# Routing with its maxima in the PSUM, high parts of the first experts beside it, two low parts moved, and filler products on TensorE

## The chip, the core and the metric

One program runs on one core of a Trainium2 chip: TensorE (PE, with its weight loads PEld), VectorE (DVE), ScalarE (ACT), GpSimd (POOL) and the queues that issue DMAs (SP's above all; ACT and POOL issue some). The metric is the time of one execution in microseconds (us); lower is better. Several executions are timed, and one more is recorded by the profiler.

## What is computed

One decoder layer: a mixer (sparse attention beside a gated linear recurrence) for 512 prompt tokens and 8 sample tokens, and behind it a mixture of 16 gated MLPs. Only the second half matters here. Cut to it:

```
h  = rms_norm(x, g_pre_ffn) * (1 + sc_f) + sh_f
pg = softmax(h @ w_rg + b_rg)                 # 4 groups of 4 experts
g_star, pg_top = argmax(pg), max(pg)
le_g = (h @ w_re + b_re) of the group g_star  # 4 logits
top_v, top_i = top_k(le_g, 2)
w_top = softmax(top_v) * pg_top               # weights of the two experts
y  = sum over the two experts e: ((silu(h @ w_gate[e]) * (h @ w_up[e])) * w) @ w_down[e]
x  = x + gt_f * rms_norm(y, g_post_ffn)
```

A token has 1024 features, an expert 256 hidden ones, so an expert's weights are 3 MB in fp32.

## The kernel before

The mixer's end runs in five token tiles of 128 (the last holds the 8 samples). `after(t, ...)` does the residual, the norm and the router's logits of tile t. Tile 3 is the last. Its final two DVE instructions are line 1376, which writes the 20 logits of each token into `LG`, and line 1377, which makes the tile's normalised rows `mg` (128x1024) for the copy `H2` in HBM, from which the experts gather.

**Routing** stands between this and the experts and runs on small tiles of 128 partitions (token in tile) by 5 tiles by a few values. `first_max` (lines 1468 to 1472) finds the first maximum in each set of four: the maximum, a comparison with it, a product with falling numbers `r4v`, its maximum, a comparison again. It is called twice (best, then second best). Line 1481 takes the best out before the second call. `OH` and `C` are the chosen experts as ones and zeros; 20 small products on TensorE with the triangle `tri` and the ones `onb` (line 1490) make every token's rank in its expert; ten products (line 1548, 16 rows) and one (line 1554) turn these into the list `gi` of rows for each expert, which GpSimd's indirect DMA (line 1615) uses to gather up to 96 rows of `H2` into a tile `XG`. The same ten products with 48 rows follow for the tokens' weights `wt`. ACT blanks the `XG` tiles (line 1575) before they are gathered into, and makes two exponentials (1480, 1498). `who` tells which expert comes at which place; SP reads it and then issues loads for experts from the fourth on.

**Experts.** TensorE multiplies fp32 as three products of a high and a low part (hi*hi, hi*lo, lo*hi). So each loaded weight tile of 128x1024 (a part: four of gate and up, two of down, numbered 6w to 6w+5 for expert w) is cut by `split`: ACT copies it to the high part (line 112), DVE or POOL subtracts that to get the low part (line 113). `split_upto(n)` cuts parts up to n. The first SOON = 4 are cut beside the routing, with their low parts on POOL; parts 4 to 7 just before the first expert, with DVE. `entry()` transposes a gathered tile on TensorE (line 1628) and splits it into `xh`, `xl`; `gate_up` is 24 products of 512 columns into one PSUM bank (line 1640); `gated`, `turned`, `down` follow.

The routing and the expert phase run in an order written by hand (`tc.manual_schedule`; for the experts the string ORD_M, where S cuts a part, G is `gate_up`, A `gated`, E `entry`, T `turned`, F `down` and the scatter, B a bit of bookkeeping, K a gather). Each engine works through its own queue in that order. Weight loads go to 28 slots; a load is issued as soon as a slot is free.

Of the kernel before, what the change touches and what calls it, by code (L numbers as in the profile page):

```python
# [39 lines left out]
HI = 12  # L40
POOLK = (2, 4, 6)
PRE = 2
SOON = 4
ONDVE = (0, 3)
CUT = (2, 4, 6)
BOOK = 0
# [18 lines left out]
def body(tc, I, O):  # L65
# [22 lines left out]
    def ps_mm():  # L88
        return bank("mm", 2, 512)
# [18 lines left out]
    def v2(t):  # L108
        return t.rearrange("p (h n) -> p h n", h=2)

    def split(src, hi, lo, eng=None):
        act.activation(hi, src, AF.Copy)  # L112
        (eng or dve).tensor_tensor(lo, src, hi.bitcast(F32), op=ALU.subtract)  # L113
# [1238 lines left out]
    def after(t, n, A, B, C, cw):  # L1352
        fast = dve if t == 3 else pool
        m = x1[t]
        xr = aft.tile([128, D], F32, name="xr", bufs=2)[:n]
        sp.dma_start(xr, I["xp"][t] if t < 4 else I["xs"])
        mg, tg = (aft.tile([128, D], F32, name=nm, bufs=2)[:n] for nm in ("mg", "tg"))
        ss = aft.tile([128, 4], F32, name="ssa", bufs=2)[:n]
        A = A()
        for hf in range(2):  # L1360
            c = slice(512 * hf, 512 * hf + 512)
            act.activation(tg[:, c], m[:, c], AF.Square, accum_out=ss[:, hf:hf + 1])
            (dve if t == 3 and hf else pool).tensor_tensor(mg[:, c], m[:, c], A[:, hf], op=ALU.mult)
        dve.tensor_scalar(ss[:, 0:1], ss[:, 0:1], 1.0 / D, EPS, op0=ALU.mult, op1=ALU.add)
        act.activation(ss[:, 1:2], ss[:, 1:2], AF.Sqrt, scale=1.0 / D, bias=ss[:, 0:1])
        dve.reciprocal(ss[:, 1:2], ss[:, 1:2])
        for hf in range(2):
            c = slice(512 * hf, 512 * hf + 512)
            dve.scalar_tensor_tensor(m[:, c], mg[:, c], ss[:, 1:2], xr[:, c], op0=ALU.mult, op1=ALU.add)
        sp.dma_start(X1[t, 0:n], m)  # L1370
        yield
        pool.tensor_tensor(v2(tg), v2(m), B(), op=ALU.mult)
        mixed[t] = act.activation(mg, m, AF.Square, accum_out=ss[:, 2:3])
        lg_ = router(tg if t == 4 else m, n, wrt if t == 4 else wrb)
        r = rstd(ss[:, 2:3])
        dve.scalar_tensor_tensor(LG[0:n, t], lg_, r, cw, op0=ALU.mult, op1=ALU.add)
        dve.scalar_tensor_tensor(v2(mg), v2(tg), r, C(), op0=ALU.mult, op1=ALU.add)
        sp.dma_start(H2[128 * t:128 * t + n], mg)

    def all_after():  # L1380
# [37 lines left out]
    def split_upto(n, lo_on=lambda c: pool if c in LOP else dve):  # L1418
        while st.cutup < n:
            i = st.cutup  # L1420
            assert i < HI or (i - HI) in used or st.over, "overwritten too early"
            load_upto(i + 1)
            at[i] = left.pop(0)
            parts[i] = high[i % HI], ring[at[i]](F32R)
            s_, raw = raws.pop(i)
            split(raw, *parts[i], lo_on(i % 6))
            left.append(s_)
            st.cutup += 1

    def source(w):  # L1430
        if w >= EARLY:
# [3 lines left out]
    tc.keep_in_program_order(act.preload_act_table_set("exp_and_others"))  # L1435
    with tc.issue_after(mixed[3].ins):
        split_upto(SOON, lambda c: pool)
    s_af.close()
    s_nsa.close()
    s_w = stage()  # L1440
# [8 lines left out]
    def small(name, *shape, dt=F32):  # L1449
        return rt.tile([128, 5, *shape], dt, name=name)  # L1450
# [2 lines left out]
        return x.unsqueeze(2).to_broadcast([128, 5, 4])  # L1453

    eg, sg_, e2 = small("eg", 4), small("sg_"), small("e2", 4)
    sets = [rt.tile([128, 25, 4], F32, name=f"sets{q}") for q in range(3)]
    mxs = [rt.tile([128, 25], F32, name=f"mxs{q}") for q in range(3)]
    C = small("C", 4, 4, dt=BF)

    def b25(x):  # L1460
# [5 lines left out]
    def first_max(x, m, oh):  # L1466

        dve.tensor_reduce(m, x, axis=AX.X, op=ALU.max)
        dve.tensor_tensor(oh, x, b25(m), op=ALU.is_equal)
        dve.tensor_tensor(oh, oh, r4v, op=ALU.mult)  # L1470
        dve.tensor_reduce(mxs[2], oh, axis=AX.X, op=ALU.max)
        dve.tensor_tensor(oh, r4, b25(mxs[2]), op=ALU.is_equal)

    lg25 = LG.rearrange("p t (g e) -> p (t g) e", e=4)
    route = tc.manual_schedule(engines={dve.engine, act.engine})
    route.__enter__()
    first_max(lg25, mxs[0], sets[0])
    mxg = mxs[0].rearrange("p (t g) -> p t g", t=5)
# [9 lines left out]
    for t in range(6):  # L1488
        for q in range(min(t, 4) + 1 if t < 5 else 5):
            pe.matmul(pr[:, 16 * t:16 * t + 16], tri if q == t else onb, C[:, q].rearrange("p g e -> p (g e)"),  # L1490
                      start=(q == 0), stop=(q == t or q == 4))
    pr = pr[:, 0:96].rearrange("p (t e) -> p t e", t=6)
    OHE = OH.rearrange("p q t g e -> p q t (g e)")
    dve.tensor_tensor(mxs[1], mxs[1], mxs[0], op=ALU.subtract)
    dve.tensor_tensor(e2, mxs[1].rearrange("p (t g) -> p t g", t=5)[:, :, 1:5], ohg, op=ALU.mult)
# [90 lines left out]
    pw = ps_t()  # L1586
    pe.matmul(pw[0:1, 0:16], kpos[0:16, 98:99], place[0:16, 0], start=True, stop=True)
    dve.tensor_copy(who, pw[0:1, 0:16])
    for q in range(2, NXG):
        blank(q)  # L1590
    weights()
# [132 lines left out]
    def fetch_upto(n):  # L1724
        while st.fetch < min(n, len(units)):
            c = units[st.fetch][1]
            fetch(gi[:, c:c + 1])
# [13 lines left out]
    with tc.manual_schedule(engines=MANUAL and {getattr(nc, e).engine for e in MANUAL}):  # L1741
        with tc.issue_after(routed[0].ins), tc.issue_after(routed[1].ins):
            fetch_upto(NXG)
            split_upto(6 + PRE)
        x, old, k = entry(), [], dict.fromkeys("GAEFTK", 0)
        fetch_upto(NXG + 1)
        for o in ORD_M:
            u = k[o] if o in k else 0
# [233 lines left out]
```

## Time and profile before

| | us |
|---|---|
| median of 3 runs (lowest to highest) | 790.48 (789.93 to 792.44) |
| the profiled execution's own time | 791.27 |
| its span, first to last instruction | 789.6 |
| busy in the span: PE, DVE, ACT, POOL | 651.7, 464.0, 374.1, 183.3 |

The profiled execution is 0.79 us above the median. Times in the rows below are from the span's start. TensorE's granted clock has two levels here, 1.0 (2.4 GHz) and 0.5 (1.2 GHz).

### The profile page before, as it was taken

The page shows a single profiled execution, that of the slowest core. Times are in us where ns is not written, and L with a number is a line of the kernel's source. Part 1 is how long each engine was busy: PE and PEld are TensorE (multiplying, and loading weights), DVE is VectorE, ACT ScalarE, POOL GpSimd, SP SyncE. Part 2 cuts the span into 40 slices and gives each one's busy share as a digit, 9 for nine tenths or more (in the row PEclk, how much of TensorE's full clock was granted, in tenths as well). Part 3 has the DMA queues.
Part 4 walks back from the last instruction along what each step waited for, and adds up shares of the span by engine and source line. Part 5 has one row for each costly group of instructions (what it writes and reads, how often), then busy time and mean ns, then how long its engine had stood idle before and what let it go on. Part 6 is the DMA issues. An engine that isn't in the chain of part 4 may idle for free. (4 is left out here: it accounts for less than half of the span.)

```text
span 789.6 us, 13169 instructions
## 1 busy us (share of the span) xinstructions
PE 651.7 (83%) x4495; PEld 490.3 (62%) x4495; DVE 464.0 (59%) x1140; ACT 374.1 (47%) x759; POOL 183.3 (23%) x208
## 2 busy tenths in 40 slices
PE   3885988998999999897999739995288899999930
PEld 1663866687878788885676426564255577666620
DVE  4523613345867765577643544356865976888806
ACT  4212512334455547623444234445445766888723
POOL 1000310002130131425432112435301223222114
PEclk9898999999999999999999958997588999999975
DMA  8876798866454632106221485338698889998515
GB/s 302 262 256 218 258 315 295 316 197 205 141 175 130 182 118 73 56 4 262 94 81 55 102 303 177 112 123 319 212 358 295 263 222 287 359 333 296 148 29 213
DMA packets 74604, 160.81 MB, mean 204 GB/s; under 512 B 11346, under 2 KB 39538, under 8 KB 74146
## 3 DMA queue, kind: packets, MB, share of 16 engines
q1 hardware_dynamic: 59844, 125.98, 46.6%
q10 hardware_dynamic: 10654, 25.39, 9.9%
q0 software_dynamic: 4032, 8.53, 5.1%
q8 instruction: 37, 0.61, 0.3%
q14 instruction: 37, 0.30, 0.1%
HBM read 145.29 MB, written 24.28 MB: 215 GB/s over the span
## 5 line engine op out<-in xcount | busy, mean ns | idle before, releaser
L563 PE MATMUL pp<-hhi,wh 128*128 128x260 f32 x256 | 75.6, 295 | 0.3 <-ACT kvt L441 0.3
L563 PE MATMUL pp<-hlo,wh 128*128 128x260 f32 x256 | 74.4, 291 | 0.0
L563 PE MATMUL pp<-hhi,wl 128*128 128x260 f32 x256 | 74.2, 290 | 0.0
L1669 POOL DMA_INDIRECT Y<-ot,gi x17 | 24.4, 1438 | 130.1 <-ACT ot L1668 123.0
L563 PEld LDWEIGHTS pp<-hhi,wh 128*128 128x128 f32 x256 | 49.4, 193 | 2.7 <-issue 2.0
L563 PEld LDWEIGHTS pp<-hhi,wl 128*128 128x128 f32 x256 | 49.3, 193 | 2.4 <-issue 2.3
L563 PEld LDWEIGHTS pp<-hlo,wh 128*128 128x128 f32 x256 | 49.4, 193 | 1.4 <-issue 1.2
L655 ACT ACTIVATE jn<-P,M 128x128 bf16<-128x128 f32 (+3 forms) x64 | 35.9, 560 | 27.3 <-DVE M L653 21.8
L113 DVE TENSOR_TENSOR wl<-wr,wh 128x1024 fp32r<-128x1024 f32 x9 | 11.2, 1250 | 39.8 <-ACT wh L112 39.8
L1058 ACT ACTIVATE PT<-mm 128x256 f32<-128x256 f32 x80 | 23.9, 388 | 19.8 <-PE mm L1054 19.7
L1640 PE MATMUL pf<-ewi,xh 128*96 128x512 f32 x72 | 30.2, 419 | 2.0 <-ACT xh L112 2.0
L653 DVE CUSTOM_DVE_ANT_0 P<-mm,tb 128x128 f32<-128x128 f32 (+3 forms) x64 | 29.0, 483 | 4.0 <-PE mm L646 3.9
L397 PE MATMUL mm<-hhi,wh 128*128 128x260 f32 x144 | 29.9, 288 | 1.3 <-ACT wh L112 1.3
L1640 PE MATMUL pf<-ewi,xl 128*96 128x512 f32 x72 | 29.5, 409 | 1.2 <-DVE xl L113 1.2
L112 ACT ACTIVATE wh<-wr 128x1024 fp32r<-128x1024 f32 x9 | 9.5, 1057 | 43.3 <-DMA wr<-in_wi 25.9
L397 PE MATMUL mm<-hlo,wh 128*128 128x260 f32 x144 | 30.0, 285 | 0.0
L397 PE MATMUL mm<-hhi,wl 128*128 128x260 f32 x144 | 29.7, 287 | 0.0
L646 PE MATMUL mm<-ka,qs 128*128 128x512 f32 (+2 forms) x112 | 27.6, 354 | 0.1
L1054 PE MATMUL mm<-qs,ka 128*128 128x512 f32 x80 | 26.6, 405 | 0.0
L1667 ACT ACTIVATE ot<-mm 96x512 f32<-96x512 f32 x17 | 10.1, 594 | 33.3 <-PE mm L1664 33.3
L397 PEld LDWEIGHTS mm<-hhi,wh 128*128 128x128 f32 x144 | 22.2, 188 | 5.0 <-issue 3.4
L299 PEld LDWEIGHTS po<-cg,w1c 128*128 128x128 f32 x160 | 21.5, 214 | 5.7 <-issue 3.3
(651 smaller groups left out, 1885.1 us busy)
## 6 DMA issues: line engine op xcount, KB each, us to landing
ewr<-in_ew SPq DMA_DIRECT2D x37, 512.0 KB
wa<-in_wa SPq DMA_DIRECT2D x16, 1024.0 KB
wr<-in_wi ACTq DMA_DIRECT2D x25, 512.0 KB
ewt<-in_ew SPq DMA_DIRECT2D x24, 512.0 KB
cg<-in_cc SPq DMA_DIRECT2D x64, 128.0 KB
ewh<-in_ew SPq DMA_DIRECT2D x16, 512.0 KB
x<-in_ew SPq DMA_DIRECT2D x15, 512.0 KB
mh<-in_wa SPq DMA_DIRECT2D x13, 512.0 KB
```

Of the source, the lines that this page charges most:

```text
L113: (eng or dve).tensor_tensor(lo, src, hi.bitcast(F32), op=ALU.subtract)
L299: pe.matmul(p[:, 128 * k:128 * k + 128], w1c[:, k, s, :], cg[:, :, k, s, :], start=(s == 0), stop=(s == 7))
L397: pe.matmul(p[:, hf, 0:260], a[:, k, :], b[:, k, hf * 260:hf * 260 + 260], start=(k == 0 and j == 0), stop=(k == KT - 1 and j == 2))
L563: pe.matmul(p[:, 0:260], a[:, k, :], b[:, k, c], start=(k == 0 and j == 0), stop=(k == KT - 1 and j == 2))
L646: pe.matmul(o, QS[g][:, h % 4, qc], KA[g][:, j, a:b], start=(j == 0), stop=(j == 1))
L653: dve.tensor_tensor_reduce(out=p, in0=sb[:, br], in1=tb0[:, 384 - 128 * i:512].rearrange("p (k n) -> p k n", n=128), scale=SL[h], scalar=1 ...
L655: act.activation(jn[:, 0:128 * (i + 1)], p.rearrange("p k n -> p (k n)"), AF.Exp, scale=-1.0, bias=M[:, 0, i, br, h:h + 1], accum_out=M[:, ...
L1054: pe.matmul(S[:, br], KS[g][:, q, br, j], QS[g][:, :, qc], start=False, stop=(q == 1))
L1058: act.activation(PT[:, :, h], S4[:, :, h], AF.Exp, scale=-SL[4 * g + h])
L1640: pe.matmul(pg, a[:, k, :], b[:, wk_], start=(k == 0 and j == 0), stop=(k == 7 and j == 2))
L1667: act.activation(o3[:, 0], pd[:, 0], AF.Copy)
L1669: pool.indirect_dma_start(out=Y, out_offset=bass.IndirectOffsetOnAxis(ap=gix, axis=0), in_=ot, in_offset=None, bounds_check=T - 1, oob_is_ ...
```

## The change

```diff
-SOON = 4
+SOON = 2
+SOONH = 6
+WARM = (5, 7, 3)
 ...
# after(t, ...)
+        if t == 3:
+            gcp = ps_mm()
+            act.activation(gcp, GC, AF.Copy)
 ...
-        dve.scalar_tensor_tensor(v2(mg), v2(tg), r, C(), op0=ALU.mult, op1=ALU.add)
+        dve.scalar_tensor_tensor(v2(mg), v2(tg), r, gcp if t == 3 else C(), op0=ALU.mult, op1=ALU.add)
 ...
# split_upto(n, lo_on)
+            high_part(i)
             s_, raw = raws.pop(i)
-            split(raw, *parts[i], lo_on(i % 6))
+            lo_on(i % 6).tensor_tensor(parts[i][1], raw, parts[i][0].bitcast(F32), op=ALU.subtract)
 ...
+    made = set()
+
+    def high_part(i):
+        if i not in made:
+            made.add(i)
+            load_upto(i + 1)
+            act.activation(high[i % HI], raws[i][1], AF.Copy)
 ...
         split_upto(SOON, lambda c: pool)
+        for i in range(SOON, SOONH):
+            high_part(i)
 ...
+    tabs = ps_f()
-    mxs = [rt.tile([128, 25], F32, name=f"mxs{q}") for q in range(3)]
+    mxs = [tabs[:, 0:25], rt.tile([128, 25], F32, name="mxs1"), tabs[:, 25:50]]
+    r4p = tabs[:, 128:228].rearrange("p (g e) -> p g e", e=4)
 ...
# first_max(x, m, oh)
-        dve.tensor_tensor(oh, oh, r4v, op=ALU.mult)
+        dve.tensor_tensor(oh, oh, r4p, op=ALU.mult)
 ...
+    junk = ps_mm().rearrange("p a b -> p (a b)")
+    def kept_up(n):
+        for _ in range(n):
+            pe.matmul(junk[:, 0:512], onb, tri.unsqueeze(1).to_broadcast([128, 4, 128]), start=True, stop=True)
+    act.activation(r4p, r4v, AF.Copy)
-    route = tc.manual_schedule(engines={dve.engine, act.engine})
+    route = tc.manual_schedule(engines={dve.engine, act.engine, pe.engine})
 ...
+    kept_up(WARM[0])        # behind the 20 rank products
 ...
+    kept_up(WARM[1])        # behind the product for `who`
 ...
             fetch_upto(NXG)
+            split_upto(SOON + 1)
+            x, old, k = entry(), [], dict.fromkeys("GAEFTK", 0)
+            kept_up(WARM[2])
             split_upto(6 + PRE)
-        x, old, k = entry(), [], dict.fromkeys("GAEFTK", 0)
```

In words: the two maxima that `first_max` writes and the numbers `r4v` that it reads lie in one PSUM bank, and for tile 3 ACT copies the table `GC` into the PSUM, from where line 1377 reads it. POOL makes two low parts beside the routing, not four; DVE makes the other two later. ACT makes six high parts beside the routing, not four. TensorE gets 5, 7 and 3 products of 512 columns whose result nobody reads. The first `entry()` comes ahead of the cutting of parts 3 to 7. How the engines' orders change shows at three places.

DVE in the routing, from line 1377 on (`tab` is the table `GC` in the SBUF, `mm` and `pf` are PSUM banks, `sets` and `mxs` SBUF tiles, `kon` and `r4v` constants in the SBUF). Before:

```order
L1377 SCALAR_TENSOR_TENSOR mg<-tg,ssa,tab_5472 128x1024
L1468 TENSOR_REDUCE mxs_6122<-LG 128x25
L1469 TENSOR_TENSOR sets_6119<-LG,mxs_6122 128x100
L1470 TENSOR_TENSOR sets_6119<-sets_6119,r4v 128x100
L1471 TENSOR_REDUCE mxs_6124<-sets_6119 128x25
L1472 TENSOR_TENSOR sets_6119<-kon,mxs_6124 128x100
L1479 TENSOR_TENSOR eg<-LG,mxs_6122 128x20
L1481 SCALAR_TENSOR_TENSOR sets_6120<-sets_6119,LG 128x100
```

The same place of the change:

```order
L1382 SCALAR_TENSOR_TENSOR mg<-tg,ssa,mm 128x1024
L1487 TENSOR_REDUCE pf<-LG 128x25
L1488 TENSOR_TENSOR sets_6120<-LG,pf 128x100
L1489 TENSOR_TENSOR sets_6120<-sets_6120,pf 128x100
L1490 TENSOR_REDUCE pf<-sets_6120 128x25
L1491 TENSOR_TENSOR sets_6120<-kon,pf 128x100
L1506 TENSOR_TENSOR eg<-LG,pf 128x20
L1508 SCALAR_TENSOR_TENSOR sets_6121<-sets_6120,LG 128x100
```

No instruction has moved; five that read two SBUF tiles now read one SBUF tile and one PSUM bank, and the last one still reads two SBUF tiles.

ACT around the routing, behind the high parts 0 to 2 (`ewi` and `mhh` are high parts, `ewr` and `ewh` loaded weights). Before:

```order
L112 ACTIVATE ewi_5426<-ewr_5837 128x1024
L1480 ACTIVATE eg<-eg 128x20
L1498 ACTIVATE mxs_6122<-mxs_6122 128x5
L1499 ACT_TABLE_LOAD
L1575 ACTIVATE XG_6106<-zero 128x1024
L1575 ACTIVATE XG_6107<-zero 128x1024
L1551 ACTIVATE oT_6201<-po 16x96
L1575 ACTIVATE XG_6108<-zero 128x1024
L1551 ACTIVATE oT_6232<-po 48x96
L112 ACTIVATE mhh_5141<-ewr_5952 128x1024
L112 ACTIVATE mhh_5142<-ewr_5954 128x1024
L112 ACTIVATE mhh_5143<-ewr_5956 128x1024
```

Of the change:

```order
L1442 ACTIVATE ewi_5426<-ewr_5837 128x1024
L1442 ACTIVATE mhh_5141<-ewr_5952 128x1024
L1442 ACTIVATE mhh_5142<-ewr_5954 128x1024
L1507 ACTIVATE eg<-eg 128x20
L1526 ACTIVATE pf<-pf 128x5
L1527 ACT_TABLE_LOAD
L1603 ACTIVATE XG_6106<-zero 128x1024
L1603 ACTIVATE XG_6107<-zero 128x1024
L1579 ACTIVATE oT_6207<-po 16x96
L1603 ACTIVATE XG_6108<-zero 128x1024
L1579 ACTIVATE oT_6245<-po 48x96
L114 ACTIVATE xh<-pt 128x384 x2
```

High parts 4 and 5 now stand ahead of the exponential `eg`, and `xh` of the first expert stands right behind the last `oT`; parts 6 and 7 follow it, where parts 4 to 7 stood ahead of it.

DVE behind the weights `wt`, at the start of the first expert. Before:

```order
L1537 TENSOR_SCALAR wt<-wt 96x16
L113 TENSOR_TENSOR ewr_6297<-ewr_5952,mhh_5141 128x1024
L113 TENSOR_TENSOR ewr_6300<-ewr_5954,mhh_5142 128x1024
L113 TENSOR_TENSOR ewr_6303<-ewr_5956,mhh_5143 128x1024
L113 TENSOR_TENSOR ewr_6306<-ewh_5958,mhh_5144 128x1024
L113 TENSOR_TENSOR xl<-pt,xh 128x384 x2
L1646 SCALAR_TENSOR_TENSOR sgx<-sgx,wt,pf 96x256
```

Of the change:

```order
L1565 TENSOR_SCALAR wt<-wt 96x16
L1432 TENSOR_TENSOR GF<-ewr_5576,ewi_5425 128x1024
L115 TENSOR_TENSOR xl<-pt,xh 128x384 x2
L1432 TENSOR_TENSOR ewr_6331<-ewr_5837,ewi_5426 128x1024
L1432 TENSOR_TENSOR ewr_6333<-ewr_5952,mhh_5141 128x1024
L1432 TENSOR_TENSOR ewr_6335<-ewr_5954,mhh_5142 128x1024
L1432 TENSOR_TENSOR ewr_6337<-ewr_5956,mhh_5143 128x1024
L1432 TENSOR_TENSOR ewr_6340<-ewh_5958,mhh_5144 128x1024
L1675 SCALAR_TENSOR_TENSOR sgx<-sgx,wt,pf 96x256
```

One low part (of part 2), not four, stands ahead of `xl`; five, not none, stand between `xl` and `sgx`.

## Rows read from the trace of the kernel before

**Rows 1.** The page of the profile: the granted TensorE clock in 40 slices of 19.7 us, in tenths of full speed.
```profile
PEclk9898999999999999999999958997588999999975
```

**Rows 2.** Busy time of each engine in stretches of 3 us: stretch, its length, PE, PEld, DVE, ACT, POOL (instructions), granted TensorE clock, busy share of the DMA engines and GB/s.
```profile
550.00:553.00 3.00, 0.00 (x0) 0.00 (x0) 2.97 (x2) 0.47 (x1) 3.00 (x2) 0.50 0.88 302
...
562.00:565.00 3.00, 1.29 (x13) 0.92 (x10) 2.04 (x13) 1.99 (x3) 0.57 (x1) 0.50 0.00 0
...
574.00:577.00 3.00, 2.42 (x6) 1.67 (x7) 0.99 (x3) 0.00 (x0) 0.00 (x0) 0.50 1.03 336
577.00:580.00 3.00, 3.00 (x14) 2.06 (x13) 0.00 (x0) 0.00 (x0) 0.00 (x0) 0.91 1.02 351
...
586.00:589.00 3.00, 3.00 (x18) 2.19 (x17) 2.97 (x6) 2.65 (x4) 0.00 (x0) 1.00 1.05 318
```

**Rows 3.** What TensorE waited for from 545 us to the end: us in total, times, longest. The listing has 13 rows; these are the first, third, fifth and eighth.
```profile
PE po L1490 <- DVE C L1486: 11.8, 1, 11.8
...
PE po L1548 <- DVE V L1519: 2.7, 1, 2.7
...
PE po L1548 <- DVE cnt L1580: 2.1, 1, 2.1
...
PE pf L1640 <- DVE xl L113: 1.2, 1, 1.2
```

**Rows 4.** The timeline of the routing, DVE and POOL: start, length, engine, line, operation, tiles, form.
```profile
546.10 2.35 POOL L113 TENSOR_TENSOR ewr<-GF,ewi 128x1024 fp32r<-128x1024 f32 x1
...
547.17 0.24 DVE L1376 SCALAR_TENSOR_TENSOR LG<-po,ssa,cW 128x20 f32<-128x20 f32 x1 [0.64 <-PE po L1331]
547.33 2.20 DVE L1377 SCALAR_TENSOR_TENSOR mg<-tg,ssa,tab 128x1024 f32<-128x1024 f32 x1
...
548.65 3.08 POOL L113 TENSOR_TENSOR ewr<-ewr,ewi 128x1024 fp32r<-128x1024 f32 x1 [0.21 <-ACT ewi L112]
...
549.73 2.12 DVE L1469 TENSOR_TENSOR sets<-LG,mxs 128x100 f32<-128x100 f32 x1
...
551.70 2.35 POOL L113 TENSOR_TENSOR GF<-ewr,ewi 128x1024 fp32r<-128x1024 f32 x1
551.89 2.28 DVE L1470 TENSOR_TENSOR sets<-sets,r4v 128x100 f32<-128x100 f32 x1
...
554.50 1.99 DVE L1472 TENSOR_TENSOR sets<-kon,mxs 128x100 f32<-128x100 f32 x1
556.41 0.17 DVE L1479 TENSOR_TENSOR eg<-LG,mxs 128x20 f32<-128x20 f32 x1
556.52 0.26 DVE L1481 SCALAR_TENSOR_TENSOR sets<-sets,LG 128x100 f32<-128x100 f32 x1
...
556.82 0.26 DVE L1468 TENSOR_REDUCE mxs<-sets 128x25 f32<-128x100 f32 x1
557.11 0.26 DVE L1469 TENSOR_TENSOR sets<-sets,mxs 128x100 f32<-128x100 f32 x1
```

**Rows 5.** The timeline before the routing: line 1377 for an earlier tile, with no POOL instruction beside it; a half tile on DVE with one operand (`mm`) in the PSUM; ACT's copy of tile 3's product; a half tile on DVE with its operands in the SBUF.
```profile
526.15 1.28 DVE L1377 SCALAR_TENSOR_TENSOR mg<-tg,ssa,tab 128x1024 f32<-128x1024 f32 x1 [0.52 <-POOL tg L1372]
...
528.28 0.74 DVE L1281 SCALAR_TENSOR_TENSOR x<-mm,rn,x 128x512 f32<-128x512 f32 x1
...
538.90 0.60 ACT L1280 ACTIVATE x<-mm 128x512 f32<-128x512 f32 x1 [1.82 <-PE mm L1277]
...
542.69 0.74 DVE L1369 SCALAR_TENSOR_TENSOR x<-mg,ssa,xr 128x512 f32<-128x512 f32 x1
```

**Rows 6.** The timeline from ACT's high parts 1 to 3 to the end of the first expert's `gate_up`.
```profile
547.52 2.95 ACT L112 ACTIVATE ewi<-ewr 128x1024 fp32r<-128x1024 f32 x3
...
567.90 2.94 ACT L112 ACTIVATE mhh<-ewr 128x1024 fp32r<-128x1024 f32 x3
...
568.72 1.54 PE L1628 MATMUL pt<-ident,XG 96*128 96x96 f32 x8
...
569.29 0.17 DVE L1537 TENSOR_SCALAR wt<-wt 96x16 f32<-96x16 f32 x1
569.40 3.53 DVE L113 TENSOR_TENSOR ewr<-ewr,mhh 128x1024 fp32r<-128x1024 f32 x3
...
571.69 0.85 ACT L112 ACTIVATE xh<-pt 128x384 fp32r<-128x384 f32 x2
...
573.98 1.01 DVE L113 TENSOR_TENSOR xl<-pt,xh 128x384 fp32r<-128x384 f32 x2
574.58 0.74 PE L1640 MATMUL pf<-ewi,xl 128*96 128x512 f32 x1 [1.20 <-DVE xl L113]
...
575.54 0.63 PE L1640 MATMUL pf<-ewr,xh 128*96 128x512 f32 x1
575.97 0.63 PE L1640 MATMUL pf<-ewi,xl 128*96 128x512 f32 x1
...
580.64 0.39 PE L1640 MATMUL pf<-ewr,xh 128*96 128x512 f32 x1
580.87 0.39 PE L1640 MATMUL pf<-ewi,xl 128*96 128x512 f32 x1
...
581.30 0.38 ACT L1645 ACTIVATE sgx<-pf 96x256 f32<-96x256 f32 x1 [8.76 <-PE pf L1640]
...
581.72 0.48 DVE L1646 SCALAR_TENSOR_TENSOR sgx<-sgx,wt,pf 96x256 f32<-96x256 f32 x1 [6.72 <-ACT sgx L1645]
```

## The prediction

> **What bounds the kernel now.** First the page's row of the granted clock [rows 1]: TensorE runs at 2.4 GHz nearly everywhere, and one of its few dips lies around slice 28 and 29, some 550 to 580 us. The table by stretches [rows 2] shows why: from 550 to 553 us TensorE does nothing while DVE and POOL are full; at 574 it works, at 1.2 GHz still; at 577 to 580 the clock comes back. By 586 everything runs at once. The list of TensorE's waits from 545 us on [rows 3] puts the time on one place: 11.8 us for `C`, the routing's result on DVE, then 2.1 and 2.7 us inside the routing and 1.2 us for `xl` of the first expert. None of its 13 rows names a DMA: behind the routing the loads come early enough, TensorE goes from product to product, and what makes the first experts start earlier should arrive at the end.
>
> The timeline of the routing [rows 4] shows what DVE does in those 11.8 us. Line 1377 takes 2.20 us, where the same form took 1.28 with POOL idle [rows 5]. Lines 1469, 1470 and 1472 take 2.12, 2.28 and 1.99 us on 100 columns; line 1469 takes 0.26 in the second call, when POOL has finished. Each long one ends about 0.1 us after a POOL low part: 551.70 + 2.35 = 554.05 on POOL, 551.89 + 2.28 = 554.17 on DVE. It works the other way too: POOL's second low part takes 3.08 instead of 2.35, since line 1377 was ahead of it. The held ones read two SBUF tiles. Line 1376 at 547.17 reads one from the PSUM (`po`), lies wholly inside POOL's first low part (546.10 to 548.45), and takes 0.24.
>
> **The routing, step by step.** Line 1377 starts at 547.33 as before, since what it waits for is unchanged. With its table in the PSUM I take 1.28 us [rows 5], so 548.6. Five steps of the first call follow at 0.29 each (556.82 to 557.11, [rows 4]), so 550.05, and `eg` at 0.11, so 550.2. Line 1481 still reads two SBUF tiles. POOL's second low part starts at 548.65, no longer delayed: it ends at 548.65 + 2.35 = 551.0. Line 1481 then ends at 551.12, and the second call starts at 551.15 instead of 556.82: 5.67 us earlier. From there POOL has no low part left and the second call was already unhindered.
>
> What an operand in the PSUM costs is bounded by two pairs: 0.24 (line 1376) against 0.17 (line 1479) for 20 columns says 0.07 us, 0.74 against 0.74 for a half tile [rows 5] says nothing. No row shows DVE writing small results to the PSUM; I take the same bounds. In the first call it is hidden in the wait for POOL (550.2 against 551.0); in the second, three instructions touch the PSUM. I take the upper bound, which small tiles are nearer to: 0.2 us. **Routing: 5.45 us earlier.** [...]
>
> ACT's copy of `GC` (1024 columns, about 1.0 us by [rows 6], 2.95 for three) stands ahead of line 1280's copy at 538.90, before which ACT idled 1.82 us [rows 5]; without that cover it would cost its 1.0. High parts 4 and 5 run on ACT from 547.52 + 2.95 = 550.5 to 552.5; behind them wait `eg` (first read in the weights) and the second exponential, due when DVE delivers it, eleven short DVE steps after the second call's start, so not before 553.4. So they cost nothing, provided that their loads have landed; the DMA engines were empty at 562 to 565 [rows 2], so nothing issued before the routing can land later than that.
>
> **The first expert, on the clock of before** (all 5.45 us earlier). The transposes start at 568.72 and `wt` is ready at 569.46 [rows 6]. Then ACT ran parts 4 to 7 until 571.7, so `xh` came at 571.69 and `xl`, behind four low parts on DVE, at 573.98; TensorE's run of products started at 574.58. In the change `xh` needs only half of the transposes: 569.5 to 570.4. DVE makes one low part, 569.46 to 570.62 (3.53 for three, 1.16 each), and `xl` from 570.6 to 571.6. TensorE's third product can start at 571.15, **3.4 us earlier**. The moved work is late next: five low parts fill DVE from 571.6 to 577.4, and `sgx` (581.72 before) queues behind them. TensorE's 22 products take 5.1 us at 2.4 GHz (0.23 apart: 580.64, 580.87) and end at 576.3, so DVE decides and `sgx` starts at 577.4, 4.3 us earlier. At 1.2 GHz they are 0.43 apart (575.54, 575.97); with as long a slow start as before (22 products in 6.7 us) they end at 577.9, and `sgx`, 0.45 behind as before, starts at 578.3, 3.4 us earlier. I take 3.9. Then DVE is the busiest engine to 592 (2.97 of 3 us in [rows 2]), and a pause of 0.3 in which its next low part waited for ACT goes. **First experts: 4.1 us earlier**, bounds 3.4 and 4.6. The two low parts that left POOL cost 2.3 us of DVE, taken out of the 6.72 us that it idled ahead of `sgx` [rows 6].
>
> **The fillers.** 15 products of 512 columns. At 1.2 GHz each takes 0.43. Five behind the rank products: 2.15 us, where TensorE waited 2.1 [rows 3]. Seven behind `who`: 3.0 us against a wait of 2.7, so 0.3 late for `wt` and the transposes behind it; at 2.4 GHz 1.6, and nothing. Three behind the transposes end before `xl`. They cost 0 to 0.3, and if the clock is up by the first expert, they are why. I read the clock as undecided, which is why 3.9 stands between its two cases.
>
> **Sum.** 5.45 + 4.1 = 9.55 us. The profiled execution's 791.27 becomes 781.7; the median stands 0.79 below it: 790.48 - 9.55 = 780.9, say **781.0**. Its own range is 779.4 (5.67 + 4.6, and 0.8 for slow clock saved later) to 782.3 (5.45 + 3.4, less 0.3 for fillers and 0.4 lost further on).
>
> **Rivals.**
> - *The PSUM operand does not take DVE out of POOL's way.* Line 1377 is held to 549.53 and line 1469 to 551.85; after that POOL is done, and line 1481 starts at about 553.0, 3.5 us earlier instead of 5.45. With the first experts' 4.1: 790.48 - 7.6 = 782.9. Against it stands line 1376, one row; for it, that its 20 columns may have slipped through. [...]
> - *The gather meets the loads.* The DMA engines are empty from 562 to 565, and the gather before ran behind that. 5.5 us earlier it follows the loads directly (0.88 busy at 550). If it lands 1.5 us later, transposes and all behind them are: 782.5.
> - *The first experts give their 4.1 back.* Weights for later experts are asked for 5.45 earlier, but used 9.5 earlier, and the DMA engines are full (1.05) at 586. For it: that fullness. Against: not one wait for a DMA in TensorE's list. Then the routing's gain alone stays: 785.0.
> - *The fillers stand in the path.* They are ahead of the routing's and the first expert's products in TensorE's queue. At 0.74 us each, the dearest product here (574.58), they are 11.1 us against 2.1 + 2.7 of waits and 0.9 ahead of `xl`: 5.4 late, 786.3. **Slower than before by 2.4 us it is from 1.18 us per filler on** ((9.55 + 2.4 + 5.7) / 15). Against it: no filler waits for anything but its turn, and the pitch of the same columns is 0.43.
>
> **How the numbers follow.** The forecast has 64 in 100, the PSUM rival 8, the gather 8, the giving back 13, the fillers 7. A difference under 0.3%, 2.4 us, can't be told from none. The first three are faster. Of giving back's 13, 3 lose so much that no change is left; of the fillers' 7, 3 are faster, 1 the same, 3 slower. So faster 0.93, same 0.04, slower 0.03. The range is 779.0 to 785.2: it holds the first three cases and most of the fourth, which leaves out some 13 in 100.
>
> **What would show it.** Right: lines 1487 to 1491 of the change at 0.25 to 0.35 us each beside POOL's second low part; line 1508 ending just after POOL at about 551; TensorE's wait for `C` down from 11.8 to about 6.3; the first run of products 8.5 to 9 us earlier, `sgx` behind DVE's low parts rather than behind TensorE; and from 600 on every row about 9.5 us earlier. Wrong: a long comparison or product in the first call; `eg` late because of the high parts; transposes that wait for `XG`; a wait of ACT for loaded weights between 570 and 600; a gap that closes later.

## The result and the profile after

The change takes 783.96 us in the median of 14 runs (778.78 to 787.33); the kernel before takes 792.38 in 14 runs beside it (786.67 to 796.32). The ratio is 0.9893, interval 0.987 to 0.9917: about 8.5 us, or 1.07%, faster. Here and below, ratios leave out slow runs, those more than 1.5% above the fastest of their kernel, and medians don't. The profiled execution of the change took 780.77 us, its span 779.0. It stands 10.5 us below the profiled one of before, but 1.88 of that lies ahead of the change: tile 3's logits (`LG`, the last row on DVE that both kernels share) were written at 547.17 before [rows 4] and at 545.29 here, and over all profiles below at 545.3 to 551.7. So every comparison from here on counts from this row. What the change adds ahead of it, ACT's copy of `GC`, does not show: from the first write of `LG` to this one it is 31.04 us before and 30.99 in the change.

The page's row of the granted clock, 40 slices, of the change:

```profile
PEclk9988999999899999999899957999698999999985
```

Where [rows 1] has 7, 5 and 8 in slices 28 to 30, it has a single 6 in slice 29 (545 to 565 us). The 8 in slice 31 (584 to 604 us) stands in both; what it costs is a matter of the rows that lie in it, further down.

The timeline of the routing of the change, DVE, POOL and TensorE (lines 1381 and 1382 answer to 1376 and 1377, lines 1487 to 1491 to 1468 to 1472, line 1508 to 1481; `pf` is the PSUM bank):

```profile
545.29 0.24 DVE L1381 SCALAR_TENSOR_TENSOR LG<-po,ssa,cW 128x20 f32<-128x20 f32 x1 [0.64 <-PE po L1333]
545.45 1.27 DVE L1382 SCALAR_TENSOR_TENSOR mg<-tg,ssa,mm 128x1024 f32<-128x1024 f32 x1
...
546.77 2.35 POOL L1432 TENSOR_TENSOR ewr<-ewr,ewi 128x1024 fp32r<-128x1024 f32 x1 [0.20 <-ACT ewi L1442]
...
546.93 0.26 DVE L1488 TENSOR_TENSOR sets<-LG,pf 128x100 f32<-128x100 f32 x1
...
547.22 0.26 DVE L1489 TENSOR_TENSOR sets<-sets,pf 128x100 f32<-128x100 f32 x1
547.52 0.27 DVE L1490 TENSOR_REDUCE pf<-sets 128x25 f32<-128x100 f32 x1
...
547.82 0.26 DVE L1491 TENSOR_TENSOR sets<-kon,pf 128x100 f32<-128x100 f32 x1
...
548.11 1.13 DVE L1508 SCALAR_TENSOR_TENSOR sets<-sets,LG 128x100 f32<-128x100 f32 x1
...
549.27 0.26 DVE L1487 TENSOR_REDUCE mxs<-sets 128x25 f32<-128x100 f32 x1
...
551.35 0.20 PE L1517 MATMUL po<-C,tri 128*128 128x16 bf16 x1 [6.09 <-DVE C L1513]
```

In [rows 4] three of the first call's rows took 2.0 to 2.3 us; here all take 0.26 or 0.27 beside POOL's second low part, and that part takes 2.35, not 3.08. Only line 1508, which still reads two SBUF tiles, waits for POOL: it ends at 549.24, POOL at 549.12. TensorE starts on `C` 6.06 us behind `LG`; before it was 11.73.

The same view at the first expert:

```profile
558.99 0.71 PE L1576 MATMUL po<-R,V 128*48 128x96 f16 x10 [1.04 <-DVE V L1547]
...
560.03 0.36 PE L1582 MATMUL po<-place,oT 48*96 48x48 f32 x2 [0.33 <-ACT oT L1579]
...
560.98 0.88 PE L1657 MATMUL pt<-ident,XG 96*128 96x96 f32 x8 [0.58 <-DMA XG<-H,gi]
...
562.30 1.01 DVE L115 TENSOR_TENSOR xl<-pt,xh 128x384 fp32r<-128x384 f32 x2
...
563.50 0.63 PE L1669 MATMUL pf<-ewi,xl 128*96 128x512 f32 x1
...
563.93 0.63 PE L1669 MATMUL pf<-ewi,xh 128*96 128x512 f32 x1
...
567.78 1.21 DVE L1432 TENSOR_TENSOR ewr<-ewh,mhh 128x1024 fp32r<-128x1024 f32 x1
...
569.25 0.39 PE L1669 MATMUL pf<-ewi,xl 128*96 128x512 f32 x1
...
570.10 0.48 DVE L1675 SCALAR_TENSOR_TENSOR sgx<-sgx,wt,pf 96x256 f32<-96x256 f32 x1 [1.11 <-ACT sgx L1674]
```

`xl` starts 17.01 us behind `LG`, before 26.81; `sgx` 24.81, before 34.55. That is 9.74 us earlier. The first products are 0.43 apart (563.50, 563.93), with the granted clock at 0.5 again (0.50 from 563.0 to 565.4 us, 1.00 from 565.6 to 569.5), and `sgx` waits 1.11 for the last product and ACT's step; DVE's last low part had ended at 568.99.

Then about 1.1 us is lost again in the third expert. The tables by stretches (PE busy first, granted clock ahead of the DMA share) and the rows of its `gate_up`, of the change:

```profile
586.00:589.00 3.00, 2.72 (x8) 1.95 (x9) 2.09 (x6) 3.00 (x5) 0.58 (x1) 0.50 1.05 350
589.00:592.00 3.00, 3.00 (x9) 1.95 (x8) 3.00 (x3) 1.02 (x2) 0.00 (x0) 0.50 0.91 299
```

```profile
580.30 0.47 DVE L1675 SCALAR_TENSOR_TENSOR sgx<-sgx,wt,pf 96x256 f32<-96x256 f32 x1
...
586.70 0.74 PE L1669 MATMUL pf<-ewi,xh 128*96 128x512 f32 x1
...
591.93 0.63 PE L1669 MATMUL pf<-ewi,xh 128*96 128x512 f32 x1
...
593.00 0.40 PE L1669 MATMUL pf<-ewi,xh 128*96 128x512 f32 x1
...
595.68 0.48 DVE L1675 SCALAR_TENSOR_TENSOR sgx<-sgx,wt,pf 96x256 f32<-96x256 f32 x1 [3.59 <-ACT sgx L1674]
```

The same rows before:

```profile
591.92 0.47 DVE L1646 SCALAR_TENSOR_TENSOR sgx<-sgx,wt,pf 96x256 f32<-96x256 f32 x1
...
598.68 0.74 PE L1640 MATMUL pf<-ewi,xh 128*96 128x512 f32 x1
...
601.36 0.45 PE L1640 MATMUL pf<-ewi,xh 128*96 128x512 f32 x1
601.64 0.40 PE L1640 MATMUL pf<-ewr,xh 128*96 128x512 f32 x1
...
606.19 0.48 DVE L1646 SCALAR_TENSOR_TENSOR sgx<-sgx,wt,pf 96x256 f32<-96x256 f32 x1 [2.10 <-ACT sgx L1645]
```

The second expert's `sgx` is still 9.74 us earlier. From it to the third's there are 15.38 us here and 14.27 before. In the change thirteen pairs of neighbours among the 24 products start 0.43 apart, before it was five; nearly all the others start 0.23 apart, and the granted clock there is 1.0 (1.00 from 593 to 596 us, before from 602 to 605). At the end of the span 8.71 us are left (233.68 us behind `LG`, before 242.39), which agrees with the 8.5 of the timed runs.

TensorE's waits from 540 us on (us in total, times, longest) confirm that no other wait took the place of those removed:

```profile
PE po L1517 <- DVE C L1513: 6.1, 1, 6.1
...
PE po L1576 <- DVE V L1547: 1.0, 1, 1.0
...
PE pt L1657 <- DMA XG<-H,gi: 0.6, 1, 0.6
```

### The profile page after: what moved, and what is told of

Read it like the earlier page. It is cut to its first block, busy times and chain, and to the rows that moved or that the text cites. A ratio compares the mean times of both kernels' runs of the same rounds, so it can differ in the third digit from the quotient of the medians.

```text
span 779.0 us, 13199 instructions
## 1 busy us (share of the span) xinstructions
PE 655.0 (84%) x4510; PEld 490.6 (63%) x4510; DVE 460.7 (59%) x1142; ACT 374.8 (48%) x761; POOL 177.9 (23%) x206
## 5 line engine op out<-in xcount | busy, mean ns | idle before, releaser
L1060 ACT ACTIVATE PT<-mm 128x256 f32<-128x256 f32 x80 | 23.9, 388 | 19.8 <-PE mm L1056 19.7
L1068 PE MATMUL po<-PT,VT 128*64 128x256 f32 x160 | 23.2, 403 | 1.8 <-POOL PT L1062 1.7
```

The lines of the kernel that those rows point to most:

```text
L1060: act.activation(PT[:, :, h], S4[:, :, h], AF.Exp, scale=-SL[4 * g + h])
L1068: pe.matmul(ob[64 * par:64 * par + 64, 256 * g:256 * g + 256], VT[:, j, br, 64 * g:64 * g + 64], PT[:, br].rearrange("p (r t) q -> p t r q ...
```

## The experiments

Four places of each trace carry the comparison, in us behind tile 3's `LG`: where TensorE starts on `C`, the first expert's `xl`, its `sgx`, the end of the span. With them stands the step from the second expert's `sgx` to the third's, and how many pairs of neighbouring products in the third expert's `gate_up` are 0.43 us apart, which goes with a granted clock of 0.5 (0.50 from 585.92 to 592.75 us in the change, from 598.60 to 601.30 before). A total that stands with a ratio was timed beside the kernel before on the same chip.

Two traces of the change differ by 0.14 to 0.38 us in the first four columns, so differences of that size are not read as effects. The end carries more of this than the rest: from the third expert's `sgx` to the last expert's all traces but one take 145.7 to 145.8 us (146.1 with the high parts late), but the stretch behind the last `sgx`, whose program no version changes, takes 37.3 to 38.4.

Of the kernel before there is one trace. The timed medians stand further below the kernel before than the traces do in most runs (11.99 us against 8.81 without fillers, 5.75 against 0.88 with the PSUM operands alone). The stretch ahead of `LG` alone differs by up to 6.4 us between the traces; what else lies in this gap stays open, and the gains below are those of the traces.

| run | `C` | `xl` | `sgx` | end | step | at 0.43 |
|---|---|---|---|---|---|---|
| before | 11.73 | 26.81 | 34.54 | 242.39 | 14.27 | 5 |
| the change | 6.05 | 17.01 | 24.80 | 233.68 | 15.38 | 13 |
| the change again | 6.19 | 17.16 | 25.13 | 234.06 | 15.30 | 10 |
| no fillers | 6.06 | 17.67 | 24.93 | 233.58 | 15.36 | 12 |
| PSUM operands alone | 9.66 | 24.70 | 33.22 | 241.51 | 14.69 | 7 |
| SBUF operands | 7.98 | 19.58 | 26.19 | 234.86 | 15.12 | 8 |
| 11 fillers for 7 | 6.06 | 17.02 | 24.90 | 233.62 | 15.38 | 13 |
| gap fillers | 6.06 | 17.02 | 24.90 | 231.28 | 12.48 | 0 |
| three more | 6.06 | 17.11 | 23.71 | 232.55 | 14.72 | 7 |
| high parts late | 6.05 | 17.02 | 24.97 | 234.26 | 15.34 | 12 |
| old order | 6.06 | 22.70 | 30.76 | 239.18 | 14.44 | 6 |
| all fillers | 6.71 | 19.56 | 26.16 | 232.43 | 12.70 | 0 |

### The PSUM operands alone

The kernel before with the tables in the PSUM, and nothing else: four low parts on POOL, no fillers, the old order (the edit against the kernel before).

```diff
+        if t == 3:
+            gcp = ps_mm()
+            act.activation(gcp, GC, AF.Copy)
...
-        dve.scalar_tensor_tensor(v2(mg), v2(tg), r, C(), op0=ALU.mult, op1=ALU.add)
+        dve.scalar_tensor_tensor(v2(mg), v2(tg), r, gcp if t == 3 else C(), op0=ALU.mult, op1=ALU.add)
...
-    mxs = [rt.tile([128, 25], F32, name=f"mxs{q}") for q in range(3)]
+    tabs = ps_f()
+    mxs = [tabs[:, 0:25], rt.tile([128, 25], F32, name="mxs1"), tabs[:, 25:50]]
+    r4p = tabs[:, 128:228].rearrange("p (g e) -> p g e", e=4)
...
-        dve.tensor_tensor(oh, oh, r4v, op=ALU.mult)
+        dve.tensor_tensor(oh, oh, r4p, op=ALU.mult)
...
+    act.activation(r4p, r4v, AF.Copy)
```

> The kernel before with the PSUM operands alone: the two maxima, the falling numbers and the table of tile 3 lie in the PSUM, GpSimd still makes four low parts, nothing else changes. Theory (an instruction with two SBUF operands waits for GpSimd's low part, one with a PSUM operand doesn't): the five instructions of the first call take 0.26 us, but the line that takes the best out still waits for the second low part, the second call's comparison (two SBUF operands) for the third and the product of the two choices for the fourth, so the first rank product comes about 9.5 us behind the logits instead of 11.73: 2.2 us faster than before. Rival (the PSUM operands alone bring the routing's gain): 6.1 behind the logits, 5.7 us faster. Second rival (they bring nothing): 11.7, no change.

Measured: 790.55 us (5 runs), ratio 0.9915 (0.9884 to 0.9946). Its routing, DVE and POOL:

```profile
552.34 2.34 POOL L113 TENSOR_TENSOR ewr<-ewr,ewi 128x1024 fp32r<-128x1024 f32 x1 [0.20 <-ACT ewi L112]
...
553.06 1.75 DVE L1487 SCALAR_TENSOR_TENSOR sets<-sets,LG 128x100 f32<-128x100 f32 x1
554.65 2.36 POOL L113 TENSOR_TENSOR GF<-ewr,ewi 128x1024 fp32r<-128x1024 f32 x1
...
555.13 1.99 DVE L1474 TENSOR_TENSOR sets<-sets,mxs 128x100 f32<-128x100 f32 x1
556.96 2.36 POOL L113 TENSOR_TENSOR ewr<-ewr,ewi 128x1024 fp32r<-128x1024 f32 x1
...
557.92 1.50 DVE L1491 TENSOR_TENSOR OH<-sets 128x80 f32<-128x80 f32 x1
```

The first call runs free beside POOL, but line 1487 behind it, line 1474 of the second call (whose `mxs` stayed in the SBUF) and line 1491, the product of the two choices, each read two SBUF tiles and are held by POOL's second, third and fourth low part. So the PSUM operands alone bring 2.07 us of the routing's 5.68. POOL's second low part started 2.09 us behind `LG` here, 1.48 before [rows 4], so up to 0.6 of what they are worth may be missing in this trace. At the end 0.88 is left, since TensorE was at the lower clock for longer in the first expert (9 pairs at 0.43, before 5) and in the third (7, before 5).

### The change with the operands in the SBUF

```diff
-        dve.scalar_tensor_tensor(v2(mg), v2(tg), r, gcp if t == 3 else C(), op0=ALU.mult, op1=ALU.add)
+        dve.scalar_tensor_tensor(v2(mg), v2(tg), r, C(), op0=ALU.mult, op1=ALU.add)
...
-    mxs = [tabs[:, 0:25], rt.tile([128, 25], F32, name="mxs1"), tabs[:, 25:50]]
+    mxs = [rt.tile([128, 25], F32, name=f"mxs{q}") for q in range(3)]
...
-        dve.tensor_tensor(oh, oh, r4p, op=ALU.mult)
+        dve.tensor_tensor(oh, oh, r4v, op=ALU.mult)
```

> The change with its operands back in the SBUF: two low parts on GpSimd, early high parts, order and fillers stay. Theory: the table's line is held until GpSimd's first low part ends, the first comparison until its second ends, and nothing after that, so the first rank product comes 8.2 us behind the logits (11.73 before, 6.06 in the change), and everything behind it 2.1 us later than in the change; the total is 2 us above the change, 6.5 below the kernel before. Rival (fewer low parts on GpSimd are the whole cause): 6.1 behind the logits, total as the change.

Measured: 786.26 us (4 runs), ratio 0.9854 (0.9812 to 0.9896). Its routing:

```profile
550.01 2.19 DVE L1379 SCALAR_TENSOR_TENSOR mg<-tg,ssa,tab 128x1024 f32<-128x1024 f32 x1
551.33 3.09 POOL L1429 TENSOR_TENSOR ewr<-ewr,ewi 128x1024 fp32r<-128x1024 f32 x1 [0.20 <-ACT ewi L1439]
...
552.41 2.13 DVE L1483 TENSOR_TENSOR sets<-LG,mxs 128x100 f32<-128x100 f32 x1
554.58 0.27 DVE L1484 TENSOR_TENSOR sets<-sets,r4v 128x100 f32<-128x100 f32 x1
```

The old pattern is back for as long as POOL works: 2.19 and 2.13 on DVE, 3.09 on POOL, and 0.27 once POOL has ended. Moving two low parts off POOL alone brings the routing 3.75 us, the PSUM operands the remaining 1.93. The two together bring about the sum of each alone (2.07 and 3.75 against 5.68). At the third `sgx` only 0.88 of the 1.93 remains, and 1.18 at the end: in the first expert `sgx` follows `xl` by 6.61 us here, by 7.79 in the change, and in the third 8 pairs are at 0.43, not 13.

### No fillers, and more of them

```diff
-WARM = (5, 7, 3)
+WARM = (0, 0, 0)
```

> The change without its 15 fillers on TensorE. Times are counted from the write of tile 3's logits (line 1376 before, 1381 in the change), so that what comes ahead of it does not count: the first rank product stood 11.73 us behind it before and 6.06 in the change, the first expert's gating on VectorE (sgx) 34.55 and 24.81. Theory: the fillers only act on TensorE's clock, so 6.06 stays, the clock stays at 1.2 GHz until some 3 us into the first expert's products as before, and sgx comes 0.3 to 1 us later than in the change (25.1 to 25.8); the total is 0 to 1 us above the change. Rival, the fillers are what brings the first experts' gain: sgx comes 2 us or more later and the total is 3 us or more above the change.

Measured: 784.31 us (4 runs), ratio 0.9839 (0.9777 to 0.9901). The transposes start 0.12 and `xl` 0.66 later without the fillers, but `sgx` only 0.13 (0.3 to 1 was expected), and the end is 0.10 earlier. In the change the clock was up ahead of the first expert (1.00 from 556 to 559 us; the seven fillers' row reads 1.68 us for seven), but down again at its first products (0.50 from 563.0 to 565.4); without the fillers it comes up in the seventh product (0.46 us long, the one before it 0.63), as in the change (0.51 and 0.63). As the change places them, they bring and cost nothing that these traces can show.

```diff
-WARM = (5, 7, 3)
+WARM = (5, 11, 3)
```

> The change with 11 instead of 7 fillers behind the product for the places. In the change the 7 ran at 2.4 GHz, took 1.68 us, and TensorE waited 1.04 us behind them; its clock fell to 1.2 GHz just as the first expert's products began. Theory: 11 fillers take 2.6 us, fill that wait, delay nothing, and the clock stays at 2.4 GHz through the first expert; its 22 products take 5.1 us instead of 6.0, sgx comes up to 1 us earlier (23.8 to 24.4 behind the logits), the total is 0 to 1 us below the change. Rival (the clock falls whatever they do, or the fillers delay the weights' products): sgx at 24.8 or later.

Measured: 785.97 us (4 runs), ratio 0.9849 (0.9812 to 0.9887). Every row in the table is within 0.1 us of the change's, and the clock falls again as the first expert's products start, 16.82 us behind `LG`; `sgx` follows `xl` by 7.88 us, in the change by 7.79. The stretch behind these fillers is what counts. There TensorE has ten small products, two more and eight transposes, with waits of 1.04, 0.33 and 0.58 us between them in the change. So the next run put three fillers into it, behind the place product for `wt`:

```diff
-WARM = (5, 7, 3)
+WARM = (5, 11, 3)
...
     for _ in first:
         pass
+    kept_up(3)
```

> The change with 11 instead of 7 fillers behind the product for the places and 3 more behind the weights' last product, ahead of the first transposes. With 11 alone the clock fell all the same, at 16.82 us behind the logits, as the first products began. Theory (the stretch of small products and transposes is what lets the clock fall): 3 more keep it up; the first expert's 22 products take 5.1 instead of 6.0 us and the first sgx comes 0.5 to 1.1 us earlier, at 23.7 to 24.4. Rival: the clock falls there again, or the fillers push the transposes; sgx at 24.8 to 25.2.

Measured: 784.84 us (one run). TensorE's rows at the first expert:

```profile
565.64 0.82 PE L1499 MATMUL mm<-tri,onb 128*128 128x512 bf16 x3
...
568.36 0.42 PE L1670 MATMUL pf<-ewi,xl 128*96 128x512 f32 x1
568.62 0.40 PE L1670 MATMUL pf<-ewi,xh 128*96 128x512 f32 x1
```

Now the products are 0.23 to 0.26 apart from `xl` on, and `sgx` comes 1.09 us earlier than in the change. The third `sgx` comes 1.97 earlier (48.42 behind `LG`): in the third expert only 7 pairs are at 0.43 (13 and 10 in the two traces of the change), though no filler was added there. So it stays up to the last expert's `sgx` (2.04). Behind it this trace has the longest end of all (38.4 us), so the end of the span comes only 1.13 earlier.

### Fillers ahead of the third expert

Six fillers behind the third expert's 16-row products and three behind its first place product, both in bookkeeping that waits for DVE and ACT between the second and the third expert.

```diff
-ORD_M = "GLAESSTBKSSSSGLAEFLSSTBBBBKSSSS...
+ORD_M = "GLAESSTBKSSSSGLAEFLSSTBWBWBBKSSSS...
...
+            elif o == "W":
+                gap.append(gap[0] if gap else ps_mm().rearrange("p a b -> p (a b)"))
+                kept_up((6, 3)[len(gap) - 1], gap[0])
```

> The change with 6 and 3 more fillers between the second expert's products and the third's (behind the ten 16-row products of the bookkeeping and behind the product for the list). Counted from tile 3's logits, the gating of experts one to four (sgx on VectorE) stands at 34.54, 44.75, 59.01, 72.39 before and at 24.80, 35.01, 50.39, 63.75 in the change: of 9.74 us only 8.62 are left from the third on, and the change's clock is at 1.2 GHz from 40.63 to 47.45, through nearly all of the third expert's 24 products, where before it was from 47.46 to 54.29, through its first seven. Theory (the loss is this slow stretch): with the waits filled the clock stays up or falls later, the third sgx comes at 47.9 to 49.5 and the end 1 to 2.4 us earlier than in the change (231.3 to 232.7 behind the logits, 233.68 in the change). Rival (the loss is something else, or the clock falls all the same): third sgx at 50.4, no gain.

Measured: 784.63 us (4 runs), ratio 0.9894 (0.9813 to 0.9974); the timed runs are too far apart to show it against the change. The trace does (a stretch, then the rows on TensorE):

```profile
592.00:595.00 3.00, 3.00 (x15) 2.15 (x15) 2.73 (x6) 3.00 (x4) 0.09 (x1) 1.00 1.05 336
```

```profile
587.65 1.47 PE L1499 MATMUL mm<-tri,onb 128*128 128x512 bf16 x6
...
589.69 0.82 PE L1499 MATMUL mm<-tri,onb 128*128 128x512 bf16 x3
...
592.06 0.47 PE L1669 MATMUL pf<-ewi,xh 128*96 128x512 f32 x1
592.37 0.39 PE L1669 MATMUL pf<-ewh,xh 128*96 128x512 f32 x1
```

The fillers hide in the waits (the first product comes 6.24 us behind the second `sgx`, in the change 6.39), the clock stays at 1.0, none of the products is at 0.43, and the step falls from 15.38 to 12.48, below the 14.27 of before. Until the second `sgx` the trace agrees with the change's to 0.1 us; at the third it is 2.80 ahead, at the end 2.40. So the 1.1 us that the change gives back is the slower clock in the third expert. The rows add up to it: eight more pairs at 0.43 instead of 0.23 are 1.6 us, and the first product comes 0.37 earlier behind the second `sgx` than before (6.39 against 6.76). By the stretches in the expectation above, the slow clock began 4.05 us ahead of the third expert's first product before and 0.78 ahead of it in the change. So before, more of the slow stretch lay in TensorE's waits. What sets where it begins, no run shows.

### The order, and the early high parts

The parts 3 to 7 cut ahead of the first `entry()`, as before the change; all else as changed.

```diff
-            split_upto(SOON + 1)
+            split_upto(6 + PRE)
             x, old, k = entry(), [], dict.fromkeys("GAEFTK", 0)
             kept_up(WARM[2])
-            split_upto(6 + PRE)
```

> The change with the order of before at the first expert: parts 2 to 7 are cut ahead of its entry, so VectorE makes six low parts before xl and ScalarE two high parts before xh. All else as in the change. Theory (the order is what brings the first expert's gain): xl comes 5.8 us later, at about 22.8 us behind the logits, the first sgx at about 29.6 (24.80 in the change, 34.54 before), the end 4.8 us above the change, at 238.5. Rival (the order matters little, since TensorE waits for the gather and the transposes): xl within 2 us of the change, end within 2.

Measured: 788.93 us (one run). Its rows:

```profile
564.45 0.85 ACT L114 ACTIVATE xh<-pt 128x384 fp32r<-128x384 f32 x2
...
566.10 3.48 DVE L1432 TENSOR_TENSOR ewr<-ewr,mhh 128x1024 fp32r<-128x1024 f32 x3
569.51 1.21 DVE L1432 TENSOR_TENSOR ewr<-ewh,mhh 128x1024 fp32r<-128x1024 f32 x1
570.64 1.01 DVE L115 TENSOR_TENSOR xl<-pt,xh 128x384 fp32r<-128x384 f32 x2
...
571.24 0.74 PE L1669 MATMUL pf<-ewi,xl 128*96 128x512 f32 x1 [4.72 <-DVE xl L115]
```

`xh` is ready at 565.3, but `xl` stands behind five more low parts on DVE, and TensorE waits 4.72 for it. The routing is the change's to 0.01 us, `sgx` comes 5.96 later (1.2 more than expected, with 7 pairs at 0.43 in the first expert) and the end 5.50. So the order carries the whole gain of the first expert. With it undone `xl` starts 16.64 us behind `C`, later than the 15.08 of before, since DVE has the two low parts that POOL no longer makes.

```diff
-SOONH = 6
+SOONH = 2
```

> The change without its early high parts of parts 2 to 5: ScalarE makes part 2's behind the routing and parts 3 to 7 behind the first expert's xh. Theory: ScalarE idles between xh and the gating of the first expert, so the high parts fit there; VectorE's low parts follow them one by one and end at about 23.6 us behind the logits, before the products do; first sgx at 24.8 to 25.2, end within 0.5 us of the change. Rival (the early high parts carry the first expert's gain): first sgx at 26.5 or later, end 2 us above the change.

Measured: 783.7 us (one run). `sgx` comes 0.17 and the end 0.58 later, not much more than two traces of the change differ by (0.33 and 0.38): the high parts beside the routing are worth little. They cost nothing: `C` is at 6.05 with them and without.

### All fillers, and the change beside them

The three more and those ahead of the third expert in one kernel, and the change again on the same chip.

```diff
-WARM = (5, 7, 3)
+WARM = (5, 11, 3)
...
+    kept_up(3)
...
-ORD_M = "GLAESSTBKSSSSGLAEFLSSTBBBBKSSSS...
+ORD_M = "GLAESSTBKSSSSGLAEFLSSTBWBWBBKSSSS...
...
```

> The change with 5, 11, 3 and 3 fillers up to the first expert and 6 and 3 between the second and third: the two fillings that, each alone, kept the clock up where they stand (first sgx 23.71 instead of 24.80 us behind the logits; third sgx 47.59 instead of 50.39, end 231.28 instead of 233.68). Theory (two separate slow stretches, each worth its products' loss): the gains add, first sgx at 23.7, third at 46.3 to 46.7, end at 230.0 to 230.6, 3.1 to 3.6 us below the change. Rival (the clock that is kept up in one place falls in another): end at 231.3 or later.

> The change itself, on the same chip as the version with all fillers, so that the two ratios to the kernel before can be set side by side. All theories: first rank product 6.05 us behind the logits, first sgx 24.8, third 50.4, end 233.7 in the profile; total 1.0 to 1.3% below the kernel before.

Measured: 778.43 us (6 runs), ratio 0.9781 (0.9734 to 0.9828); the change 785.29 (6 runs), ratio 0.9854 (0.98 to 0.9909). The ratios are 0.73% apart, about 5.8 us, and the intervals overlap only from 0.98 to 0.9828: this version is the fastest here. Its profiled execution took 782.55, 4.1 above its median, and by its end shows only 1.6 us of this. TensorE's rows there:

```profile
560.20 4.63 PE L1499 MATMUL mm<-tri,onb 128*128 128x512 bf16 x11
...
566.65 0.82 PE L1658 MATMUL pt<-ident,XG 96*128 96x96 f32 x8
```

In this execution the clock came up only behind the eleven fillers. They took 4.63 us together, 0.42 each (2.55, 0.23 each, with three more fillers), and the products for `wt` behind them and the transposes came late: the transposes 18.25 us behind `LG`, in the change 15.68. (0.66 of that was lost earlier: POOL's second low part started 2.13 behind `LG`, in the change 1.48.) So the gains did not add as expected: the end is at 232.43, not at 230.0 to 230.6. The first `sgx` (26.16) is 1.36 later than in the change, not 1.1 earlier. The third expert's gain came in full (a step of 12.70, no pair at 0.43) and makes up for it. Where the rest of the 5.8 us comes from no trace shows.

## Why the prediction was right, and where it was off

**The total.** Forecast were 781.0 us and 779.0 to 785.2; measured 783.96. Of the 2.96 between them 1.90 is the kernel before, whose median over 14 runs is 792.38, not the 790.48 of three. The difference itself was forecast at 9.55 and is 8.5 in the timed runs, 8.71 in the traces.

**The routing: right.** Forecast 5.45 us, measured 5.68. (One reading was too wide: the held lines of 100 columns end 0.1 us behind a low part, but line 1377 ended 1.08 behind one, at 549.53 against 548.45.) The second call was to start 3.98 us behind `LG` (551.15 less 547.17) and does (549.27 less 545.29). The 0.2 us for operands in the PSUM is the part that was too much: line 1382 takes 1.27 against 1.28 for line 1377 unhindered [rows 5], and the first call's five steps take 0.26 or 0.27 with the PSUM, and 0.26 or 0.27 with the SBUF where POOL is idle (line 1484 above, [rows 4] at 556.82), so the lower bound, nothing, was the true one. In the routing of before, of the change and of the two runs that split it, DVE's steps with two SBUF inputs are held while POOL makes a low part (1.13 to 2.3 us, line 1508 and [rows 4]), and those with one input in the PSUM aren't (0.26 or 0.27 us on 100 columns, 1.27 on 1024).

**The first expert: size right, reason half right.** Forecast 3.9, measured 4.06 by `sgx`. `xl` was to start 17.98 us behind `LG` (570.6 less the 5.45 and less 547.17) and started at 17.01. That is 0.97 ahead of the forecast; 0.66 of it goes without the fillers, so that much is the small products and transposes at the upper clock (the transposes take 0.88 us, 1.54 without the fillers), which the sum had on the clock of before. DVE's low parts then ended 1.1 earlier too (23.70 behind `LG`, forecast 24.78), and TensorE, not DVE, decided `sgx`: its first products ran at the granted clock 0.5, 0.43 apart. The text had both cases and stood between them. That 3.9 came so near is in part luck: the clock was the slow case's, which the sum had at 3.4, but the third product started 0.32 us earlier than reckoned (18.21 behind `LG`, not 18.53), and from it to `sgx` there were 6.60 us, not 7.15. That the order decides is shown by the run with the old one. The prediction's 2.4 and 1.2 GHz stand for the granted clock's 1.0 and 0.5; what the runs show are these levels and the pitch of products of 512 columns at each, 0.23 and 0.43 us, and no frequency.

**After the first expert: this step failed.** "I take 3.9. Then DVE is the busiest engine to 592 [...] and a pause of 0.3 in which its next low part waited for ACT goes", which made 4.1 of it; and "from 600 on every row about 9.5 us earlier". Measured, the step from the first `sgx` to the second is 10.20 us, before 10.21: the 0.2 did not come. And the third expert loses 1.11, for which the sum had no term; the fillers ahead of it show that this is the clock (13 pairs of products 0.43 us apart, before five, with those fillers none). In the list of rivals the giving back was one of weights and full DMA engines. It did happen, at a quarter of its price, and by another mechanism: TensorE's list of waits has no DMA but 0.6 for `XG`. The profile of before held a sign of it: its products in the third expert, too, began at the lower clock (598.68 to 601.36 in its timeline, 0.43 apart; the granted clock is 0.50 from 598.60 to 601.30), and the prediction read the clock only up to the first expert.

**The sum as measured**: 5.68 and 4.06 gained, 1.11 given back, 0.08 gained further on: 8.71.

**Fillers: right.** They cost nothing, as forecast (0 to 0.3). The clock was left undecided; it was not up at the first expert's first products, so they bought nothing there either. The rival in which they stand in the path did not come true in the change, but in part in the kernel with all fillers.

**Gather: right.** The transposes start 5.87 us earlier, more than `C`, so the gather did not meet the loads; the wait for `XG` is 0.6 us.

## What to carry to other kernels

Where DVE's small steps last 2 us beside GpSimd, give them one operand in the PSUM (here 0.26 or 0.27 us then) or take the work off GpSimd; here it took both to free the chain, all but one step, and a held small step is found by its end, 0.1 us behind GpSimd's. When a chain is shortened, look at which of TensorE's products then fall under the lower clock, also an expert or two later: part of the gain may be lost again there, without any wait in the list. Here fillers paid in the last gaps ahead of the products that they were for; ahead of small products that others wait for they bought nothing, and in one trace, where they took 0.42 us each, delayed the transposes by some 2 us.

## What the runs showed of the hardware that was not expected

- GpSimd gains, too: its low part takes 2.35 us beside DVE's PSUM operands and 3.08 or 3.09 behind the line that makes `mg` (1377 before) with two SBUF inputs.
- DVE's results of 25 columns go to the PSUM (line 1490, 0.27 us) as fast as to the SBUF (line 1487 in the second call, 0.26).
- The same instructions ran at either level of the clock. The kernels with three more fillers and with all fillers have the same instructions up to the first expert; in one the eleven fillers took 2.55 us, in the other 4.63. The two traces of the change differ too (13 and 10 pairs at 0.43 in the third expert).
- Nine products of 512 columns that nobody reads, 2.3 us in all, removed the one fall of the clock behind the first expert, up to 750 us: with the gap fillers the mean granted clock is 1.00 from 572 to 750 us, in the change it is 0.50 from 585.92 to 592.75.
